# Raw buffers of their own for the modulation's weights, a fourth buffer for the high parts, and unread products in bfloat16

## The chip, the cores and the metric

The kernel runs on one core of a Trainium2 chip. The metric is the device time of one execution in microseconds (us). The kernel before was timed in 3 runs: 2639.55, 2638.19 and 2629.68 us, median 2638.19 us.

## The reference, cut to what matters

Two blocks are run one after the other in float32 on 256 tokens of 1024 channels. The first has two layers with four branches (RWKV-7, latent attention, a convolution, cross-attention to a memory). The second has two layers of a gated feed-forward, a mixed attention and another gated feed-forward, on the 256 tokens and on 256 context tokens. What each of its sublayers shifts, scales and gates is computed from the conditions `c` and `c_ctx` by one wide matrix per layer, the modulation:

```python
def first_block(x, ...):                      # two layers; every product has weights of its own
    for l in range(DEPTH):
        h = x @ w_in[l]
        ...
        merged = jnp.sum(gates * proj, axis=2)
        x = _layer_norm(DEEPNORM_ALPHA * x + merged @ w_out[l], ln_g[l], ln_b[l])
    return x

def swiglu(h, w1, w2):
    gate, up = jnp.split(h @ w1, 2, axis=-1)
    return (jax.nn.silu(gate) * up) @ w2

def ffn_sublayer(h, m, sub, g_pre, g_post, w1, w2):
    shift, scale, gate = mods_of(m, sub)
    y = swiglu(modulate(rms_norm(h, g_pre[sub]), shift, scale), w1, w2)
    return h + MACARON_WEIGHT * gate * rms_norm(y, g_post[sub])

def second_block(x, c, ctx, c_ctx, w_mod, b_mod, ...):
    xc = ctx
    c_act = jax.nn.silu(c)
    cc_act = jax.nn.silu(c_ctx)
    for layer in range(DEPTH):
        mod = (c_act @ w_mod[layer] + b_mod[layer]).reshape(b, 1, N_MOD, D_MODEL)
        mod_c = (cc_act @ w_mod[layer] + b_mod[layer]).reshape(N_MOD, D_MODEL)
        x, xc = hybrid_layer(x, xc, mod, mod_c, ...)   # ffn (sub 0), attention (sub 1), ffn (sub 2)
    return x
```

`mod` has 9 parts of 1024 numbers for each layer, three (shift, scale, gate) for each of the sublayers 0, 1 and 2. They depend on `c` alone, so they can be computed at any time before the sublayer that reads them.

## The kernel before, in words

**Weights.** All products are made in two parts, because TensorE multiplies a float32 operand rounded. A weight tile of 128 x 1024 float32 (512 KB) goes through `wload` (L178): SyncE (SP) issues a DMA into a raw buffer `wr` (pool of 4, L183), ScalarE (ACT) casts it to the high part `wh` (pool of 3, L175), and VectorE (DVE) subtracts to get the low part `wl` (pool of 3, L176). TensorE (PE) then makes three products for each pair of operands: high by high, high by low, low by high (`gemm`, L192). The kernel has 547 such tiles; they are numbered here in the order in which they are split. A tile of the feed-forward on 512 columns (256 tokens and 256 context tokens, tiles 240 to 300 for the first one) is 24 matmuls of 128x512. A raw buffer can be loaded again once its cast and its subtraction are done; a buffer of high parts, once TensorE has used it.

**Modulation.** It is computed in two ways. Layer 0's sublayer 0 goes through `mods` (L1212): 24 tiles of `wmod` are loaded in pairs, and TensorE multiplies them without a split; this runs beside the first block's second layer. The other five sublayers go through `mods_rows` (L1166), beside the second block: a 512 KB tile of the transposed matrix, `wmodT`, is fetched (L1173), and VectorE multiplies it by the row of silu(c) and sums along each row (L1188), once for the tokens and, in 88 of the 120 tiles, once more for the context. This document calls one such instruction a sum; there are 208. Each writes its 1024 products to `prod`, which is never read, and the sum to a column of `mm`, which is what counts. The fetch of the next tile stands right behind the sums of the last one. Both ways take their raw buffers from the same pool `wr` as the weights, and both are generators that `tick` (L214), called at the end of each `wload`, moves on by one step, so that their instructions are written between those of the tiles; `MODS_GAPS` sets after how many ticks the next tile follows.

**Order.** The program is compiled with a scheduler that moves instructions on each engine by its own costs and by when buffers come free; what it decides is then fixed. At run time each engine, and SP's queue of DMAs too, takes its instructions strictly in that order: one that waits holds up all behind it on its engine. Names in the rows: `ac`, `rw`, `sm` and `md` are PSUM accumulators; `blk`, `u`, `u2`, `u4`, `yout`, `pt` are tiles of activations; `ah` and `al` are the high and low parts of an activation.

**Lines.** L1224 is the fetch in `mods`, L1161 an activation in `c_rows` (L1154) that uses `prod` as a scratch tile, L1262 and L1275 open the second block's pools; the feed-forward's eviction is at L1466 to L1468.

Of the kernel before, what the change touches and what calls it, by code (L numbers as in the profile page):

```python
# [9 lines left out]
F32 = mybir.dt.float32  # L10
F32R = mybir.dt.float32r
BF16 = mybir.dt.bfloat16
I32 = mybir.dt.int32
AF = mybir.ActivationFunctionType
# [143 lines left out]
class Build:  # L158
    def __init__(self, tc, ap):
        self.tc, self.nc, self.ap = tc, tc.nc, ap  # L160
        self.bg = []
        self.ticks = 0
        self.modded = set()


# [11 lines left out]

    def wload(self, src, n, pieces=1):  # L178
        nc = self.nc
        raw = self.wr.tile([128, 1024], F32, name="wr")  # L180
        for p in range(pieces):
            sl = slice(p * n // pieces, (p + 1) * n // pieces)
            nc.sync.dma_start(out=raw[:, sl], in_=src[:, sl])  # L183
        h = self.wh.tile([128, 1024], F32R, name="wh")
        l = self.wl.tile([128, 1024], F32R, name="wl")
        for p in range(pieces):
            sl = slice(p * n // pieces, (p + 1) * n // pieces)
            self.split(h[:, sl], l[:, sl], raw[:, sl])
        self.tick()
        return h, l  # L190
# [43 lines left out]
    def build(self):  # L234
        nc, tc, ap = self.nc, self.tc, self.ap
        with ExitStack() as st:
            pool = lambda name, bufs, **k: st.enter_context(tc.tile_pool(name=name, bufs=bufs, **k))
            self.dr = pool("dr", 1, space=DRAM)
            self.wr = pool("wr", 4)
            self.wh = pool("wh", 3)  # L240
            self.wl = pool("wl", 3)
            c = self.c = pool("c", 1)
            self.ident = c.tile([128, 128], F32, name="ident")
            nc.scalar.dma_start(out=self.ident, in_=ap["ca"][:, 0:128])
            self.mhalf = c.tile([128, 16], F32, name="mhalf")
            nc.gpsimd.memset(self.mhalf, -0.5)
            self.ac = pool("ac", 2, space=PSUM)
            self.rw = pool("rw", 2, space=PSUM)
            self.sm = pool("sm", 3, space=PSUM)
            self.md = pool("md", 1, space=PSUM)  # L250
            self.accs = [self.ac]

            with ExitStack() as fin:
                with ExitStack() as s1:
                    self.first(fin, s1)
                self.second_open(st)
                self.finish(L - 1)
            self.second(st)


    def first(self, fin, st):
        nc, tc, ap = self.nc, self.tc, self.ap
        pool = lambda name, bufs, **k: st.enter_context(tc.tile_pool(name=name, bufs=bufs, side="right", **k))
        self.fin = fin.enter_context(tc.tile_pool(name="fin", bufs=1))
        self.ts = fin.enter_context(tc.tile_pool(name="ts", bufs=4))
        p1 = self.p1 = pool("p1", 1)
        self.ts.tile([128, 32], F32, name="pad3", bufs=1)
        self.f4 = fin.enter_context(tc.tile_pool(name="f4", bufs=7))
        self.xth = self.fin.tile([128, 8, 256], F32R, name="xth")
        self.xtl = self.fin.tile([128, 8, 256], F32R, name="xtl")  # L270
        self.ahead = []
        for k in range(0, 8, 2):
            xt = self.four((128, 2, 256))
            nc.sync.dma_start(out=xt, in_=ap["xT"][128 * k : 128 * k + 256].rearrange("(k p) t -> p k t", p=128))
            self.split(self.xth[:, k : k + 2], self.xtl[:, k : k + 2], xt)
            if k == 0:
                self.ahead.append(self.wload(ap["win"][0, :, 0:1024], 1024, 2))
        self.t1 = pool("t1", 2)
        self.t2 = pool("t2", 2)
        self.d2 = pool("d2", 16)  # L280
        self.d4 = pool("d4", 5)
        self.rp = pool("rp", 1)
        self.lw = p1.tile([128, 256], F32, name="lw")
        self.xd = self.dr.tile([256, 1024], F32, name="xd")
        for l in range(L):
            self.layer(l)
# [867 lines left out]
    def c_rows(self):  # L1154

        nc = self.nc
        self.cr = self.p2.tile([128, 2, 1024], F32, name="cr")
        self.prod = self.p2.tile([128, 1024], F32, name="prod")
        for r in range(2):
            nc.sync.dma_start(out=self.cr[:, r], in_=self.ap["cR"][r].partition_broadcast(128))  # L1160
            nc.scalar.activation(self.prod, self.cr[:, r], AF.Tanh, scale=0.5)  # L1161
            nc.vector.scalar_tensor_tensor(out=self.cr[:, r], in0=self.prod, scalar=1.0, in1=self.cr[:, r], op0=ALU.add,
                                           op1=ALU.mult)
            nc.vector.tensor_scalar(out=self.cr[:, r], in0=self.cr[:, r], scalar1=0.5, scalar2=None, op0=ALU.mult)

    def mods_rows(self, *which):  # L1166
# [2 lines left out]
        V = nc.vector  # L1169

        def fetch(l, sub, g):
            raw = self.wr.tile([128, 1024], F32, name="wr")
            nc.sync.dma_start(out=raw, in_=ap["wmodT"][l, sub, :, 1024 * g : 1024 * g + 1024])  # L1173
            return raw

# [36 lines left out]
    def mods(self, *which):  # L1212
# [3 lines left out]
        for l, sub in which:  # L1216
            for blk in range(6 * sub, 6 * sub + 6):
                m, half = blk // 2, slice(512 * (blk % 2), 512 * (blk % 2) + 512)
                ps = self.md.tile([128, 512], F32, name="md")
                for i in range(0, 4, 2):  # L1220
                    u = 4 * blk + i
                    raw = [self.wr.tile([128, 1024], F32, name="wr") for _ in range(2)]
                    for j in range(2):
                        nc.sync.dma_start(out=raw[j], in_=ap["wmod"][l, :, 1024 * (u + j) : 1024 * (u + j) + 1024])  # L1224
                    yield

                    for k in range(4):
                        self.mm(ps[32 * k : 32 * k + 32], self.cs[:, 2 * i + k],
                                raw[k // 2][:, 512 * (k % 2) : 512 * (k % 2) + 512], i == 0, i == 2)
                    yield  # L1230
                mr = self.wr.tile([128, 1024], F32, name="wr")
                A.copy(mr[:, 0:512], ps)
                for r in range(2):
                    nc.scalar.dma_start(out=self.ms[l, sub][r, :, m % 3, half], in_=mr[r:128:32, 0:512])
                yield

            q = self.wr.tile([128, 1024], F32, name="wr")
            nc.sync.dma_start(out=q[:, 0:80], in_=ap["pmod"][l, sub])
            gd = self.gd[l, sub]
            for r in range(2):  # L1240
# [21 lines left out]
    def second_open(self, st):  # L1262
        nc, ap = self.nc, self.ap
        pool = lambda name, bufs: st.enter_context(self.tc.tile_pool(name=name, bufs=bufs, side="right"))
        self.accs = [self.ac, self.rw]
        self.us = pool("us", 4)

        pool("pad", 1).tile([128, 48], F32, name="pad")
        self.xc = pool("xc", 1).tile([128, 2, 1024], F32, name="xc")
        nc.sync.dma_start(out=self.xc, in_=ap["ctx"].rearrange("(t p) d -> p t d", p=128))  # L1270
        self.u2 = pool("u2", 4)
        self.u4 = pool("u4", 3)
        self.blk = pool("blk", 5)

    def second(self, st):  # L1275
        nc, tc, ap = self.nc, self.tc, self.ap
        pool = lambda name, bufs, **k: st.enter_context(tc.tile_pool(name=name, bufs=bufs, **k))
        p2 = self.p2 = pool("p2", 1)
        p2.tile([128, 16], F32, name="pad2")
        self.ah = pool("ah", 4)  # L1280
        self.pt = pool("pt", 4)
        self.cb = p2.tile([128, NCB], F32, name="cb")
        nc.sync.dma_start(out=self.cb, in_=ap["cb"])
        for n, (a, b) in CB.items():
            setattr(self, n, self.cb[:, a:b])
        for l in range(L):
            last = l == L - 1
            if l == 0:
                self.c_rows()
                self.bg.append((self.mods_rows((0, 1), (0, 2), (1, 0), (1, 1), (1, 2)), 1))  # L1290
            self.ffn(l, 0, 0, (0, 1) if l else (1, 0), (l, 1))
            self.attention(l, last)
            self.ffn(l, 1, 2, (0,) if last else (0, 1), None if last else (l + 1, 0))
        for t in range(2):
            for c, queue in enumerate((nc.sync, nc.scalar)):
                sl = slice(512 * c, 512 * c + 512)
                queue.dma_start(out=ap["out"][128 * t : 128 * t + 128, sl], in_=self.X[0][t][:, sl])
# [535 lines left out]
```

## Time and profile before

| | |
|---|---|
| time, median of 3 runs | 2638.19 us (2629.68 to 2639.55) |
| the profiled execution's own time | 2642.53 us |
| its span, first to last instruction | 2640.7 us |
| mean granted TensorE clock | 0.989 |
| busy: PE, DVE, ACT, POOL | 2542.3, 1763.3, 1133.0, 231.2 us |
| DMA: moved, mean rate | 384.82 MB, 146 GB/s |
| DVE idle ahead of a sum, for its `wmodT` tile | 301.4 us, 93 times |

The profile gives for each engine the time in which it was busy, and for each instruction what ended the idle time before it. TensorE's matmuls are pipelined and their ends are modelled, so how far apart two matmuls start tells more than the length of one. The granted clock is full (1.00, the level of 2.4 GHz) or half (1.2 GHz); a stretch that mixes them shows a mean between.

### The profile page before, as it was taken

The page shows a single profiled execution, that of the slowest core. Times are in us where ns is not written, and L with a number is a line of the kernel's source. Part 1 is how long each engine was busy: PE and PEld are TensorE (multiplying, and loading weights), DVE is VectorE, ACT ScalarE, POOL GpSimd, SP SyncE. Part 2 cuts the span into 40 slices and gives each one's busy share as a digit, 9 for nine tenths or more (in the row PEclk, how much of TensorE's full clock was granted, in tenths as well). Part 3 has the DMA queues.
Part 4 walks back from the last instruction along what each step waited for, and adds up shares of the span by engine and source line. Part 5 has one row for each costly group of instructions (what it writes and reads, how often), then busy time and mean ns, then how long its engine had stood idle before and what let it go on. Part 6 is the DMA issues. An engine that isn't in the chain of part 4 may idle for free.

```text
span 2640.7 us, 42329 instructions
## 1 busy us (share of the span) xinstructions
PE 2542.3 (96%) x16658; PEld 2167.7 (82%) x16658; DVE 1763.3 (67%) x3066; ACT 1133.0 (43%) x1936; POOL 231.2 (9%) x245
## 2 busy tenths in 40 slices
PE   8999999998999899999899999999999999899998
PEld 7888998877899888887766788887788888766997
DVE  7988667797766785557777575656654445655656
ACT  5365454444545532233546342223432234545445
POOL 1121101112111100000212010000000000111000
PEclk9999999999999999999999999999999999999999
DMA  6344466545547654444441244444445543322564
GB/s 206 105 120 137 131 207 217 155 134 194 158 121 217 199 185 138 152 158 145 128 128 56 82 153 157 147 155 143 146 147 157 160 128 96 96 80 85 171 185 151
DMA packets 124712, 384.82 MB, mean 146 GB/s; under 512 B 28352, under 2 KB 32176, under 8 KB 124384
## 3 DMA queue, kind: packets, MB, share of 16 engines
q1 hardware_dynamic: 121504, 380.19, 47.2%
q8 instruction: 131, 2.15, 0.3%
q10 hardware_dynamic: 3008, 1.92, 0.2%
q14 instruction: 69, 0.57, 0.1%
HBM read 379.80 MB, written 2.26 MB: 145 GB/s over the span
## 4 chain that ended last, share of the span: by engine, by line
PE 71%; DVE 13%; DMA 7%; issue 4%; ACT 2%; POOL 1%; DVEq 0%; SPq 0%; POOLq 0%; ACTq 0%
PE ac L167 37%; PE rw L167 20%; PE sm L167 10%; DMA wr<-in_wmodT 6%; DVE wl L176 4%; PE md L167 2%; PE sm L170 2%; DVE prod L1188 2%; DVE br L816 2%; DMA wr<-in_win 1%; ACT wh L175 1%; POOL rs L204 1%; DVE blk L1351 0%; DVE br L1424 0%; PE rw L170 0%
## 5 line engine op out<-in xcount | busy, mean ns | idle before, releaser
L175 ACT CAST wh<-wr 128x1024 fp32r<-128x1024 f32 (+2 forms) x547 | 569.0, 1041 | 852.7 <-PE ac L167 388.2
L176 DVE TENSOR_TENSOR wl<-wr,wh 128x1024 fp32r<-128x1024 f32 (+2 forms) x547 | 696.9, 1275 | 240.0 <-ACT wh L175 237.3
L1188 DVE CUSTOM_DVE_ANT_0 prod<-wr,cr 128x1024 f32<-128x1024 f32 x208 | 254.2, 1222 | 302.5 <-DMA wr<-in_wmodT 301.4
L167 PE MATMUL rw<-blk,wh 128*128 128x512 f32 (+1 forms) x1600 | 424.6, 350 | 4.2 <-DVE blk L1350 3.8
L167 PE MATMUL ac<-blk,wh 128*128 128x512 f32 (+1 forms) x1552 | 412.9, 351 | 2.6 <-DVE blk L1350 1.8
L167 PE MATMUL ac<-xth,wh 128*128 128x256 f32 x1248 | 356.9, 286 | 7.6 <-ACT wh L175 5.3
L167 PE MATMUL ac<-xth,wl 128*128 128x256 f32 x1248 | 350.1, 281 | 2.6 <-DVE wl L176 2.4
L167 PE MATMUL ac<-xtl,wh 128*128 128x256 f32 x1248 | 349.4, 280 | 0.1
L167 PEld LDWEIGHTS rw<-blk,wh 128*128 128x128 f32 x1600 | 283.3, 189 | 45.0 <-DVE blk L1350 4.7
L167 PEld LDWEIGHTS ac<-blk,wh 128*128 128x128 f32 x1552 | 275.6, 190 | 42.0 <-DVE blk L1350 2.3
L167 PE MATMUL rw<-blk,wl 128*128 128x512 f32 (+1 forms) x800 | 279.7, 350 | 4.5 <-DVE wl L176 4.5
L167 PE MATMUL ac<-blk,wl 128*128 128x512 f32 (+1 forms) x776 | 272.2, 351 | 1.1 <-DVE wl L176 1.1
L167 PEld LDWEIGHTS ac<-xth,wh 128*128 128x128 f32 x1248 | 236.2, 189 | 18.1 <-issue 7.6
L167 PEld LDWEIGHTS ac<-xth,wl 128*128 128x128 f32 x1248 | 235.9, 189 | 5.6 <-DVE wl L176 4.2
L167 PEld LDWEIGHTS ac<-xtl,wh 128*128 128x128 f32 x1248 | 236.1, 189 | 2.5 <-issue 1.5
L175 ACT CAST ah<-blk 128x512 fp32r<-128x512 f32 (+1 forms) x170 | 95.8, 566 | 195.7 <-PE sm L167 98.6
L167 PEld LDWEIGHTS rw<-blk,wl 128*128 128x128 f32 x800 | 151.0, 189 | 25.1 <-DVE wl L176 5.7
L167 PEld LDWEIGHTS ac<-blk,wl 128*128 128x128 f32 x776 | 146.9, 189 | 21.2 <-DVE wl L176 1.9
L176 DVE TENSOR_TENSOR al<-blk,ah 128x512 fp32r<-128x512 f32 (+1 forms) x170 | 103.9, 619 | 64.7 <-ACT ah L175 64.6
L816 DVE SCALAR_TENSOR_TENSOR br<-hp,pv,br 128x256 f32<-128x256 f32 x240 | 113.8, 508 | 0.9
L167 PE MATMUL ac<-f,wh 128*128 128x256 f32 x640 | 113.9, 280 | 0.0
L204 POOL TENSOR_TENSOR rso<-rso,mhalf 128x1 f32<-128x1 f32 x20 | 15.5, 773 | 1001.8 <-DVE rso L1419 1001.8
(440 smaller groups left out, 4257.9 us busy)
## 6 DMA issues: line engine op xcount, KB each, us to landing
wr<-in_w SPq DMA_DIRECT2D x264, 512.0 KB
wr<-in_win SPq DMA_DIRECT2D x187, 512.0 KB
wr<-in_wmodT SPq DMA_DIRECT2D x120, 512.0 KB
wr<-in_wo SPq DMA_DIRECT2D x32, 512.0 KB
wr<-in_wout SPq DMA_DIRECT2D x32, 512.0 KB
wr<-in_wmod SPq DMA_DIRECT2D x24, 512.0 KB
wr<-in_wkv SPq DMA_DIRECT2D x16, 512.0 KB
gate<-gd SPq DMA_DIRECT2D x10, 512.0 KB
```

Source lines behind the costliest of these rows:

```text
L167: self.nc.tensor.matmul(out, a, b, start=start, stop=stop, skip_group_check=True)
L170: self.nc.tensor.transpose(out, a, self.ident[:n, :n])
L175: nc.scalar.copy(h, src)
L176: (eng or nc.vector).tensor_tensor(out=l, in0=src, in1=h.bitcast(F32), op=ALU.subtract)
L204: self.nc.gpsimd.tensor_tensor(out=out, in0=in_, in1=self.mhalf[:p, :n], op=ALU.pow)
L816: V.scalar_tensor_tensor(out=acc, in0=hp[:, j : j + 256], scalar=w(j), in1=acc, op0=ALU.mult, op1=ALU.add)
L1188: V.tensor_tensor_reduce(out=self.prod, in0=raw, in1=self.cr[:, r], scale=1.0, scalar=0.0, op0=ALU.mult, op1=ALU.add, accum_out=m[:, g, r ...
```

## The change

Three things are changed. The pool of raw buffers has 3 instead of 4, and that of high parts 4 instead of 3; in the first block every fourth weight tile goes to one more raw buffer, `wx`, which is dropped when the second block is opened. The modulation takes its tiles from a pool of its own: 2 buffers (`w0`) in `mods`, 1 buffer (`wm`) in `mods_rows`. And the products that nobody reads, `prod`, become bfloat16 (the scratch of `c_rows` moves to a `yout` tile).

```diff
@@ Build.__init__
+        self.wx, self.turn = None, 0
@@ wload
-        raw = self.wr.tile([128, 1024], F32, name="wr")
+        self.turn = (self.turn + 1) % 4
+        raw = (self.wx if self.wx and self.turn == 0 else self.wr).tile([128, 1024], F32, name="wr")
@@ build
-            self.wr = pool("wr", 4)
-            self.wh = pool("wh", 3)
+            self.wr = pool("wr", 3)
+            self.wh = pool("wh", 4)
@@ first
+        self.wx = pool("wx", 1)
+        self.wm = pool("w0", 2)
@@ c_rows
-        self.prod = self.p2.tile([128, 1024], F32, name="prod")
+        tmp = self.yout().rearrange("p a t -> p (a t)")
+        self.prod = self.p2.tile([128, 1024], BF16, name="prod")
@@ mods_rows, fetch
-            raw = self.wr.tile([128, 1024], F32, name="wr")
+            raw = self.wm.tile([128, 1024], F32, name="wm")
             nc.sync.dma_start(out=raw, in_=ap["wmodT"][l, sub, :, 1024 * g : 1024 * g + 1024])
@@ mods
-                    raw = [self.wr.tile([128, 1024], F32, name="wr") for _ in range(2)]
+                    raw = [self.wm.tile([128, 1024], F32, name="wr") for _ in range(2)]
...
-                mr = self.wr.tile([128, 1024], F32, name="wr")
+                mr = self.wm.tile([128, 1024], F32, name="wr")
...
-            q = self.wr.tile([128, 1024], F32, name="wr")
+            q = self.wm.tile([128, 1024], F32, name="wr")
@@ second_open
+        self.wx = None
@@ second
+        self.wm = pool("wm", 1)
```

The scheduler also writes the instructions in another order. Three places follow; in the rows, a number behind a name tells one tile from another, and a line of after stands 2 to 7 higher than the same line of before.

SP's queue in the first feed-forward of the second block, around weight tile 253, before:

```order
L183 DMA wr_12122<-in_w1 128x1024
L1173 DMA wr_12130<-in_wmodT 128x1024
L183 DMA wr_12157<-in_w1 128x1024
L183 DMA wr_12192<-in_w1 128x1024
L1173 DMA wr_12200<-in_wmodT 128x1024
L183 DMA wr_12227<-in_w1 128x1024
```

The same queue at the same tile, after:

```order
L185 DMA wr_12134<-in_w1 128x1024
L1178 DMA wm_12072<-in_wmodT 128x1024
L185 DMA wr_12169<-in_w1 128x1024
L1178 DMA wm_12142<-in_wmodT 128x1024
L185 DMA wr_12204<-in_w1 128x1024
L1178 DMA wm_12212<-in_wmodT 128x1024
L185 DMA wr_12239<-in_w1 128x1024
```

Fetches and weight loads stand about 2 to 3 before and 1 to 1 after, and a fetch stands behind a later weight load than it did (`wm_12142` behind tile `wr_12169`; before, the same tile of the modulation, `wr_12130`, behind `wr_12122`).

VectorE at the same place, before (rows with `mm` alone read the sum out):

```order
L176 TENSOR_TENSOR wl_12125<-wr_12122,wh_12124 128x1024
L1188 ISA prod_11354,mm_11380<-wr_12200,cr_11353 128x1024
L1188 ISA mm_11380 128x1
L176 TENSOR_TENSOR wl_12160<-wr_12157,wh_12159 128x1024
L1467 SCALAR_TENSOR_TENSOR u2_12118<-u2_12118,ac_12062 128x512
L1188 ISA prod_11354,mm_11380<-wr_12235,cr_11353 128x1024
L1188 ISA mm_11380 128x1
L1188 ISA prod_11354,mm_11380<-wr_12235,cr_11353 128x1024
L1188 ISA mm_11380 128x1
```

And after:

```order
L177 TENSOR_TENSOR wl_12137<-wr_12134,wh_12136 128x1024
L1193 ISA prod_11366,mm_11392<-wm_12212,cr_11364 128x1024
L1193 ISA mm_11392 128x1
L1193 ISA prod_11366,mm_11392<-wm_12212,cr_11364 128x1024
L1193 ISA mm_11392 128x1
L177 TENSOR_TENSOR wl_12172<-wr_12169,wh_12171 128x1024
L1474 SCALAR_TENSOR_TENSOR u2_12130<-u2_12130,ac_12074 128x512
L1193 ISA prod_11366,mm_11392<-wm_12247,cr_11364 128x1024
L1193 ISA mm_11392 128x1
L1475 SCALAR_TENSOR_TENSOR blk_11376<-u2_12130,rw_12105 128x512
L177 TENSOR_TENSOR wl_12207<-wr_12204,wh_12206 128x1024
L1193 ISA prod_11366,mm_11392<-wm_12247,cr_11364 128x1024
```

Between tiles 240 and 300 VectorE has 76 sums before and 104 after; a pair of sums on one tile of the modulation now stands at nearly each weight tile, with one or two other instructions between a pair's end and the next pair.

VectorE at the end of the first attention of the second block (weight tile 319), before:

```order
L176 TENSOR_TENSOR ah_14096<-sm_15700,al_14095 128x256
L1721 SCALAR_TENSOR_TENSOR blk_14089<-sm_15739,blk_14089 128x256
L1721 SCALAR_TENSOR_TENSOR blk_14089<-sm_15746,blk_14089 128x256
L176 TENSOR_TENSOR ah_14096<-sm_15778,al_14095 128x256
L176 TENSOR_TENSOR wl_15864<-wr_15861,wh_15863 128x1024
L1188 ISA prod_11354,mm_15770<-wr_15995,cr_11353 128x1024
```

And after:

```order
L1193 ISA prod_11366,mm_17534<-wm_17456,cr_11364 128x1024
L1193 ISA mm_17534 128x1
L177 TENSOR_TENSOR ah_14108<-sm_15712,al_14107 128x256
L1728 SCALAR_TENSOR_TENSOR blk_14101<-sm_15751,blk_14101 128x256
L1728 SCALAR_TENSOR_TENSOR blk_14101<-sm_15758,blk_14101 128x256
L1193 ISA prod_11366,mm_17534<-wm_17540,cr_11364 128x1024
L1193 ISA mm_17534 128x1
L1193 ISA prod_11366,mm_17534<-wm_17540,cr_11364 128x1024
L1193 ISA mm_17534 128x1
L177 TENSOR_TENSOR ah_14108<-sm_15790,al_14107 128x256
L177 TENSOR_TENSOR wl_15876<-wr_15873,wh_15875 128x1024
L1193 ISA prod_11366,mm_17534<-wm_17610,cr_11364 128x1024
```

There, between tiles 310 and 320, VectorE has 12 sums before and 32 after. The last sum stands at tile 434 before and at tile 369 after.

## Rows read from the trace of the kernel before

**Rows 1.** The page: engines' busy time, and the chain that ended last.

```profile
PE 2542.3 (96%) x16658; PEld 2167.7 (82%) x16658; DVE 1763.3 (67%) x3066; ACT 1133.0 (43%) x1936; POOL 231.2 (9%) x245
...
PE 71%; DVE 13%; DMA 7%; issue 4%; ACT 2%; POOL 1%; DVEq 0%; SPq 0%; POOLq 0%; ACTq 0%
```

**Rows 2.** Waits, whole program: engine, line, releaser; us in total, times, longest.

```profile
DVE prod L1188 <- DMA wr<-in_wmodT: 301.4, 93, 6.7
```

**Rows 3.** Waits of SP's own queue, whole program.

```profile
SPq L183 <- DMA wr<-in_wmodT: 170.1, 59, 4.5
```

**Rows 4.** Waits of DVE between 930 and 1212 us (tiles 239 to 290).

```profile
DVE prod L1188 <- DMA wr<-in_wmodT: 100.4, 26, 6.7
DVE wl L176 <- ACT wh L175: 1.3, 3, 0.8
```

**Rows 5.** Busy time by stretch: PE, PEld, DVE, ACT, POOL (instructions), PEclk, DMA share, GB/s.

```profile
500.00:700.00 200.00, 184.40 (x1819) 154.41 (x1818) 170.34 (x400) 91.90 (x185) 40.61 (x49) 0.98 0.51 163
930.00:1212.00 282.00, 276.29 (x1211) 226.10 (x1209) 179.80 (x258) 78.63 (x97) 0.14 (x1) 1.00 0.50 157
1212.00:1340.00 128.00, 118.99 (x586) 99.90 (x586) 98.83 (x148) 58.78 (x103) 13.99 (x9) 0.97 0.50 148
1340.00:1483.00 143.00, 140.68 (x676) 93.00 (x676) 94.71 (x297) 79.97 (x197) 27.21 (x23) 1.00 0.24 69
1483.00:1512.00 29.00, 29.00 (x129) 23.81 (x128) 14.14 (x19) 7.65 (x15) 0.57 (x1) 1.00 0.42 135
1610.00:1770.00 160.00, 160.00 (x708) 132.38 (x707) 94.31 (x136) 39.29 (x46) 0.14 (x1) 1.00 0.48 152
1770.00:1830.00 60.00, 56.23 (x240) 45.12 (x239) 38.49 (x56) 21.51 (x30) 0.00 (x0) 0.97 0.50 151
1895.00:1910.00 15.00, 11.56 (x62) 9.80 (x62) 12.82 (x26) 9.93 (x22) 3.22 (x4) 0.89 0.35 106
```

**Rows 6.** DVE's groups by shape: count | busy us, mean ns | idle before.

```profile
L1188 DVE CUSTOM_DVE_ANT_0 prod<-wr,cr 128x1024 f32<-128x1024 f32 x208 | 254.2, 1222 | 302.5 <-DMA wr<-in_wmodT 301.4
...
L1467 DVE SCALAR_TENSOR_TENSOR u<-u,ac 128x512 f32<-128x512 f32 x44 | 29.9, 680 | 1.9 <-ACT u L1466 1.9
```

**Rows 7.** SP's DMA issues from 975 us: start, us, line (x2: two issues merged).

```profile
981.39 0.33 SPq L1173 DMA_DIRECT2D wr<-in_wmodT  x1
983.13 4.84 SPq L183 DMA_DIRECT2D wr<-in_w  x2
988.78 0.33 SPq L1173 DMA_DIRECT2D wr<-in_wmodT  x1
```

**Rows 8.** DVE in order of time, near 985 and 2501 us: start, us, [idle before <-releaser].

```profile
981.28 0.08 DVE L1188 DVE_READ_ACCUMULATOR2_ANT mm<- 128x1 f32 x1
...
985.11 1.23 DVE L1188 CUSTOM_DVE_ANT_0 prod<-wr,cr 128x1024 f32<-128x1024 f32 x1 [2.01 <-DMA wr<-in_wmodT]
...
987.53 1.22 DVE L176 TENSOR_TENSOR wl<-wr,wh 128x1024 fp32r<-128x1024 f32 x1
...
993.99 1.23 DVE L1188 CUSTOM_DVE_ANT_0 prod<-wr,cr 128x1024 f32<-128x1024 f32 x1 [4.64 <-DMA wr<-in_wmodT]
...
2501.53 1.23 DVE L176 TENSOR_TENSOR wl<-wr,wh 128x1024 fp32r<-128x1024 f32 x1 [0.54 <-ACT wh L175]
```

**Rows 9.** PE in order of time, near 1210 and 1825 us.

```profile
1210.60 0.50 PE L167 MATMUL ac<-wl,ah 128*128 128x512 f32 x1 [2.84 <-DVE wl L176]
...
1212.95 0.80 PE L167 MATMUL ac<-wh,al 128*128 128x512 f32 x1 [0.78 <-DVE al L176]
...
1825.80 0.51 PE L167 MATMUL rw<-wl,ah 128*128 128x512 f32 x1 [3.12 <-DVE wl L176]
```

**Rows 10.** ACT in order of time, last feed-forward.

```profile
2500.45 1.05 ACT L175 CAST wh<-wr 128x1024 fp32r<-128x1024 f32 x1 [1.50 <-PE rw L167]
...
2508.93 1.05 ACT L175 CAST wh<-wr 128x1024 fp32r<-128x1024 f32 x1 [1.78 <-PE ac L167]
...
2511.75 1.05 ACT L175 CAST wh<-wr 128x1024 fp32r<-128x1024 f32 x1 [1.50 <-PE rw L167]
```

More of the change, by code (lines that the diff above doesn't have):

```diff
@@ L1157, in c_rows @@
         self.cr = self.p2.tile([128, 2, 1024], F32, name="cr")
-        self.prod = self.p2.tile([128, 1024], F32, name="prod")
+        tmp = self.yout().rearrange("p a t -> p (a t)")
+        self.prod = self.p2.tile([128, 1024], BF16, name="prod")
         for r in range(2):
             nc.sync.dma_start(out=self.cr[:, r], in_=self.ap["cR"][r].partition_broadcast(128))
-            nc.scalar.activation(self.prod, self.cr[:, r], AF.Tanh, scale=0.5)
-            nc.vector.scalar_tensor_tensor(out=self.cr[:, r], in0=self.prod, scalar=1.0, in1=self.cr[:, r], op0=ALU.add,
+            nc.scalar.activation(tmp, self.cr[:, r], AF.Tanh, scale=0.5)
+            nc.vector.scalar_tensor_tensor(out=self.cr[:, r], in0=tmp, scalar=1.0, in1=self.cr[:, r], op0=ALU.add,
                                            op1=ALU.mult)
```

## The prediction, made before the run

> **What bounds the kernel now.** First the page: TensorE is busy for 96% of the span and the chain that ended last runs through it for 71% [rows 1]. What the change can give back is therefore no more than TensorE's idle time and half clock, and what it can cost is whatever makes TensorE wait longer. Then the waits: VectorE idles 301.4 us ahead of the modulation's sums, for a `wmodT` tile [rows 2], and weight loads stand in SP's queue for 170.1 us behind such a tile's buffer [rows 3]. Most of that costs TensorE nothing as long as VectorE keeps its place, so I read by stretch. From 930 to 1212 us VectorE waits 100.4 us for `wmodT` and 1.3 us for anything else [rows 4]: it never waits for the casts, so it is late already, its queue being sums, subtractions and waits for fetches. TensorE still loses only 282 - 276.29 = 5.7 us there [rows 5], much of it in one place, 2.84 + 0.78 us at 1210 [rows 9]. So in the first feed-forward of the second block VectorE and TensorE run side by side with next to no slack; there the change puts more sums. From 1610 to 1770 TensorE is busy throughout; 160 us / 708 = 0.226 us per matmul, and 24 of them make 5.4 us per weight tile [rows 5].
>
> **Single buffer in the first feed-forward (tiles 240 to 300).** The order has 104 sums in 60 tiles, 52 fetches, where it had 76. With one buffer a fetch can only start when the second sum on the last tile has read it. A cycle is then: the sum read out at 981.28 + 0.08, the issue at 981.39, 0.33 us long, so the DMA leaves at 981.72 and its sum starts at 985.11: 3.39 us; two sums from 985.11 to 987.53: 2.42 us [rows 7, 8]. Together 0.03 + 0.33 + 3.39 + 2.42 = 6.2 us, above the 5.4 us of a weight tile. What VectorE does between a pair and the next (a subtraction of 1.22 us, an eviction of 0.68 [rows 6, 8]) lies inside the 3.39 us. But in about nine pairs such work stands between the two sums, and there it lengthens the cycle by 1.22 + 0.68 = 1.9 us, 17 us in all. 52 x 6.2 + 17 = 339 us, against 60 x 5.4 = 325 us of TensorE and, with the 4 us at 1210, about 329 us before: **+10 us**. From below: if VectorE's lead at the start (up to two low parts, 11 us) covers it, 0. From above: the tile issued at 988.78, about 1 us behind a weight load, starts its sum at 993.99, 4.9 us after its issue ends [rows 7, 8]; a cycle of 7.7 us would give 52 x 7.7 + 17 - 329 = +88 us. I take the lower landing, because in the new order the fetch stands directly ahead of the weight load that waits for the next subtraction, as at 981.39 (the two loads behind it begin at 983.13), and not behind it.
>
> The Trainium skill ("DMA: Bandwidth & Descriptors", Anatomy of one DMA) gives a fixed 2.0 us plus bytes / 436 GB/s for a DMA issued from GpSimd. For 512 KB that is an estimate of 3.2 us, near the 3.39 us seen on SP's queue; the sum by it would be 10 us lower, so no loss in this stage. It says nothing of the 4.9 us seen behind another load, and the trace has both.
>
> **Transition and attention (tiles 300 to 330).** At tile 300 the order has one pair more, 2.4 us and a wait on a path where TensorE already loses 128 - 118.99 = 9.0 us [rows 5]: +3 us (0 to +6). Between tiles 310 and 320 there are 32 sums for 12: 20 x 1.22 = 24 us of work and ten more fetches of up to 3.4 us exposed, 58 us at most. VectorE's idle time there is 172 - 108.9 = 63 us of the stretch from 1340 to 1512, and TensorE loses only 2.3 us in it [rows 5]. Much of that idle time is at the end, where the high and low parts of the output wait for one another, and there the new order puts four pairs back to back with three to five short instructions between, each with its fetch bare. Four pairs at 5.8 us less the hidden work and the idle time that was there leave some 14 us: **+14 us** (0 if the idle time takes it all, +35 if the pairs stand bare before the projection). Behind that, to tile 369, there is one sum per weight tile, and a cycle of 6.2 us for two tiles is hidden in 10.8: 0.
>
> **What goes.** Behind tile 369 no sums are left. At 1825.80 TensorE waits 3.12 us for a low part, and the stretch to 1830 loses 3.8 us and 0.03 x 60 = 1.8 us of clock [rows 5, 9]: -6 us (bounds -6 and 0). From 1895 to 1910 TensorE idles 3.4 us, with VectorE busy 12.8 of 15 us [rows 5] and one sum among it: -2 us. Beside the first block's second layer, weight loads no longer stand behind the modulation's pairs in one ring and stand 3 to 4 tiles ahead in the order instead of 1; TensorE idles 15.6 us between 500 and 700 [rows 5], a third of which I give to it: -5 us (-12 to +5, since SP's queue is in order and a pair now waits there for TensorE to have read the last one). Each new gap of over 3 us also drops the clock to half for a while, as before 1830: three new gaps at 1.8 us: +5 us.
>
> **What costs nothing.** Three raw buffers in the last feed-forward: a cast comes every 2.82 us and a subtraction ends at 2502.76; with four buffers the next load into it is cast at 2511.75, with three at 2508.93 [rows 8, 10]. That leaves 6.2 us, above the 4.9 us of the slowest landing used here; without that cover, each of its narrow tiles would wait. The fourth high part lets a cast run one tile earlier, but in this part casts wait for TensorE and nothing waits for them: 0. bfloat16 products: a sum takes 1222 ns for 1024 columns [rows 6], the same as a subtraction of two float32 tiles, so I read one column per cycle set by the two float32 inputs: 0, and -0.6 us per sum at best.
>
> The sum against the profiled execution's 2642.5 us: 10 + 3 + 14 - 6 - 2 - 5 + 5 = +19, that is 2661.5 us. That execution was 4.3 us above the median of the runs, 2638.2 us, so **2657 us** beside that median.
>
> **Rivals.**
> *The fetch hides at last (faster).* The buffer is the modulation's own, so a fetch no longer waits in a ring for a weight tile's subtraction, and a weight load no longer waits for a sum. For it: 301.4 and 170.1 us of waits [rows 2, 3]. Against it: one buffer is one fetch in flight at best, and never under a sum. If lead and idle time hide the three additions, what goes is left, and with it 1210 and half of the idle time from 1212 to 1340: -13 - 6 - 5 = -24, beside the median 2614 us.
> *Contended landing (much slower).* The single buffer's cycle is not 6.2 us but midway to the row of 4.9 us, 6.9 us: 52 x 6.9 + 17 - 329 = +47 in place of +10, so about 2694 us. It decides from a landing of 4 us on; the row at 988.78 is for it.
> *All of it beside TensorE (no change).* 96% busy, and the losses and the gains are of one size: 2638 us. For it: TensorE lost only 5.7 us in 282 with VectorE late throughout.
> *Cheaper sums.* The Trainium skill ("VectorE: DVE Perf Modes", Terms) has the engine pick its mode from the operands' types and alignment, with more than one result per cycle from 16 bits; no row here shows a sum with a 16-bit output. As a mechanism of this kernel: a sum of 0.6 us makes the cycle 5.0 us, 52 x 5.0 + 17 = 277 us, below TensorE's 325, so it ends like the first rival, about 2612 us. The two inputs stay float32, which speaks against it.
>
> **How the numbers follow.** Forecast as worked out 0.42, with a range of its own of 2643 to 2674; contended 0.14; no change 0.20; fetch hides 0.19; cheaper sums 0.05. About 0.5%, 13 us, is what a measurement of this kernel can tell from no change. The forecast's range reaches 8 of its 42 hundredths into that band. So faster 0.19 + 0.05 = 0.24; same 0.20 + 0.08 = 0.28; slower 0.34 + 0.14 = 0.48. The range, 2612 to 2694 us, leaves out the longer half of the contended case and a little of the faster ones.
>
> **What would show it.** Right: between tiles 240 and 300 VectorE's waits for `wm` grow in number to about 52, each near 1.5 us (3.4 less 1.9 of hidden work), TensorE gets waits for `wl` there (over 10 us) and the stage grows from 329 to about 339 us; from tile 310 to 320 TensorE's idle time grows from 2 to about 16 us; behind tile 369 VectorE waits for nothing of the modulation, and the gap at 1825 is gone. Wrong: sums of 0.6 us; a fetch that lands over 4 us after its issue throughout; SP's weight loads waiting for raw buffers in the last feed-forward; or a first feed-forward as long as before, whose VectorE waits for casts.

## The result, and the profile after

The changed kernel takes 2652.4 us (median of 5 runs, 2646.0 to 2655.7), the kernel before 2638.19 us (median of 5, 2629.68 to 2641.25). The ratio is 1.0052, 95% interval 1.0034 to 1.0070: half a per cent slower. The profiled execution took 2650.9 us with a span of 2649.1 us, 8.4 us more than the one of before.

Page of after, busy time and the chain that ended last, to be held against [rows 1]:

```profile
PE 2547.8 (96%) x16658; PEld 2170.9 (82%) x16658; DVE 1754.7 (66%) x3066; ACT 1133.2 (43%) x1936; POOL 248.5 (9%) x245
...
PE 59%; DVE 9%; DMA 8%; issue 3%; POOL 1%; ACT 1%; DVEq 0%; POOLq 0%; ACTq 0%; SPq 0%
```

Waits of after, whole program (engine, line, releaser; us in total, times, longest), to be held against [rows 2]:

```profile
DVE prod L1193 <- DMA wm<-in_wmodT: 150.6, 94, 3.4
ACT wh L176 <- DMA wr<-in_w: 145.7, 68, 6.1
```

VectorE's wait for the modulation's tiles is halved, 301.4 us in 93 times to 150.6 in 94, and the kernel is slower. The sum of a wait over the program says nothing here; the stretch does.

TensorE runs the same products in nearly the same order in all these kernels, so the start of the same matmul in two traces can be subtracted. What a kernel gains or loses on before from one milestone to the next (us, worked out that way; times at the head are those of before, columns are stretches, and `end` is the total):

```
                          to 456 456-667 667-700 700-937 937-1271 1271-1331 1331-1512 1512-1770 1770-1843 1843-2451 2451-2575  end
after                        0.0    -3.5    +7.0    -4.4    +12.8      -1.0     +10.7      +0.3      -7.8      -1.4      -4.7  +8.0
own_buffer_wr4_wh3          +1.1    -5.7    -1.1    +1.8    +15.3      -0.8      +8.5      +3.5      -7.8      -1.7       0.0 +13.2
three_high_parts            -0.4    -5.9    -1.2    -1.3    +12.5      +1.4      +5.1      +1.2      -7.8      -2.0       0.0  +1.6
two_buffers_wh3             -1.1    -7.1    -0.7    +0.8     +4.1      -3.5      +6.3      -3.1      -7.8      -1.8       0.0 -13.9
paced_one_buffer            +2.2    -3.5    +5.9    -5.3     -7.8      -0.6      +5.2      +2.1      -7.8      +1.1       0.0  -8.5
paced_three_high_parts      +1.4    -8.2    -0.5    +1.6     -6.3      +5.1      +7.9      +1.8      -7.8      -0.8      -4.6 -10.2
paced_two_buffers           -0.3    -5.9    -0.5    +1.7    -10.6      -2.0      +5.0      +4.9      -7.8      -2.7      -4.6 -22.9
one_sum_per_fetch           +0.4    -7.0    +7.0    -4.5    -10.4      -4.6      +3.0      +0.4      -7.8      +1.4      -4.6 -26.8
before_bf16_only            +1.2    +0.8    -0.2    +5.2     -4.6      -2.1      +2.8      -0.3       0.0      +0.3      -4.6  -1.4
```

The first row is the result; the others are the experiments below. The first feed-forward of the second block (937 to 1271) lost 12.8 us, the attention (1331 to 1512) 10.7 us, a place at 667 to 700 7 us; 1770 to 1843 and the last feed-forward gave back 7.8 and 4.7 us. The last row shows how far one profile can be trusted: `before_bf16_only` runs TensorE's products in exactly the order of before, and yet its stretches differ from before's by up to 5.2 us. An entry of that size in a single profile is not to be put down to a change; 12.8 us is well clear of it, and -7.8 us comes out alike in eight kernels. One column does not go with the change at all: in 2451 to 2575 each kernel shows either 0 or -4.6 us, and `before_bf16_only` shows -4.6 (last section). Without it the profile's difference is 12.7 us, close to the medians' 14.2.

Busy time of after by stretch (columns as in [rows 5]); the second row is the first feed-forward, the fourth the attention:

```profile
660.00:700.00 40.00, 35.19 (x274) 31.21 (x271) 27.39 (x69) 16.67 (x33) 4.74 (x4) 0.91 0.41 122
936.00:1283.00 347.00, 332.69 (x1430) 268.44 (x1429) 247.22 (x362) 99.41 (x130) 0.28 (x2) 0.99 0.55 170
1283.00:1342.00 59.00, 51.16 (x298) 44.40 (x297) 49.48 (x76) 32.24 (x62) 17.74 (x9) 0.97 0.45 126
1342.00:1534.00 192.00, 186.47 (x845) 128.71 (x844) 142.31 (x374) 90.44 (x215) 28.91 (x24) 0.96 0.37 113
1792.00:1852.00 60.00, 60.00 (x266) 49.72 (x265) 26.20 (x32) 23.23 (x35) 0.00 (x0) 1.00 0.31 92
```

The same matmuls of the first feed-forward in before:

```profile
937.00:1271.00 334.00, 327.51 (x1430) 268.27 (x1429) 215.79 (x308) 100.67 (x132) 0.14 (x1) 0.99 0.50 158
```

334 us became 347, TensorE's idle time in it went from 6.5 us to 14.3; the rest shows as longer matmuls beside the waits (busy 332.7 us against 327.5), of which about 1.7 us are half clock: the trace's records of the granted clock have 6.8 us at the lower level here in after and 3.4 in before. Who it waits for, and whom VectorE waits for (after, 936 to 1283 us):

```profile
PE ac L168 <- DVE wl L177: 6.7, 7, 1.3
PE ac L168 <- DVE al L177: 6.2, 6, 2.2
```

```profile
DVE prod L1193 <- DMA wm<-in_wmodT: 95.4, 49, 3.4
```

49 waits of 95.4 / 49 = 1.95 us each, for 51 tiles of the modulation (102 sums in this trace between tiles 240 and 300, two fewer than the 104 given with the change). The cycle can be read off VectorE in order of time (after):

```profile
1103.03 1.23 DVE L1193 CUSTOM_DVE_ANT_0 prod<-wm,cr 128x1024 bf16<-128x1024 f32 x1 [2.02 <-DMA wm<-in_wmodT]
1104.18 0.08 DVE L1193 DVE_READ_ACCUMULATOR2_ANT mm<- 128x1 f32 x1
1104.30 1.22 DVE L1193 CUSTOM_DVE_ANT_0 prod<-wm,cr 128x1024 bf16<-128x1024 f32 x1
1105.45 0.08 DVE L1193 DVE_READ_ACCUMULATOR2_ANT mm<- 128x1 f32 x1
1105.45 1.22 DVE L177 TENSOR_TENSOR wl<-wr,wh 128x1024 fp32r<-128x1024 f32 x1
1106.59 0.68 DVE L1474 SCALAR_TENSOR_TENSOR u<-u,ac 128x512 f32<-128x512 f32 x1
1109.51 1.23 DVE L1193 CUSTOM_DVE_ANT_0 prod<-wm,cr 128x1024 bf16<-128x1024 f32 x1 [2.24 <-DMA wm<-in_wmodT]
...
1115.62 1.23 DVE L1193 CUSTOM_DVE_ANT_0 prod<-wm,cr 128x1024 bf16<-128x1024 f32 x1 [1.27 <-DMA wm<-in_wmodT]
...
1121.72 1.23 DVE L1193 CUSTOM_DVE_ANT_0 prod<-wm,cr 128x1024 bf16<-128x1024 f32 x1 [1.86 <-DMA wm<-in_wmodT]
```

And SP's issues at that time (after):

```profile
1105.56 0.33 SPq L1178 DMA_DIRECT2D wm<-in_wmodT  x1
1106.70 0.33 SPq L185 DMA_DIRECT2D wr<-in_w  x1
1112.04 0.33 SPq L1178 DMA_DIRECT2D wm<-in_wmodT  x1
```

The sum's read-out ends at 1105.53, the fetch is issued at 1105.56 to 1105.89, and the next sum starts 3.6 us later, at 1109.51; the next one 3.25 us after its issue ends (1112.37 to 1115.62). These three cycles are 6.5, 6.1 and 6.1 us long, against 5.4 us of TensorE's weight tile [rows 5], and the one subtraction that TensorE needs lies inside each.

Worked out in the same way from SP's issues and VectorE's rows, the 51 cycles of the stretch follow one another without a break, each fetch issued 0.03 us behind the last read-out. From 939.47 on they take 347.1 us, as long as the whole stretch: 6.8 us each. 31 of them take 6.0 to 6.7 us. Of the 20 longer ones eleven have other work of VectorE between the two sums, eight a late landing, and in one VectorE was busy elsewhere when the tile came. The eight are the fetches that were issued 1.1 to 1.7 us behind a weight load: their sum starts 4.4 to 4.7 us after the issue ends. The fetches issued 3 us or more behind one took 3.2 to 4.0 us, apart from the one for which VectorE was busy.

### The profile page after: what moved, and what is told of

Same layout as the page of the kernel before. It is cut to its first block, busy times and chain, and to the rows that moved or that the text cites. A ratio compares the mean times of both kernels' runs of the same rounds, so it can differ in the third digit from the quotient of the medians.

```text
span 2649.1 us, 42312 instructions
## 1 busy us (share of the span) xinstructions
PE 2547.8 (96%) x16658; PEld 2170.9 (82%) x16658; DVE 1754.7 (66%) x3066; ACT 1133.2 (43%) x1936; POOL 248.5 (9%) x245
## 4 chain that ended last, share of the span: by engine, by line
PE 59%; DVE 9%; DMA 8%; issue 3%; POOL 1%; ACT 1%; DVEq 0%; POOLq 0%; ACTq 0%; SPq 0%
PE ac L168 27%; PE rw L168 19%; PE sm L168 9%; DMA wm<-in_wmodT 8%; DVE prod L1193 4%; PE md L168 3%; PE sm L171 2%; DVE wl L177 1%; DVE br L820 1%; POOL rs L206 1%; DVE br L1431 0%; DVE u L1338 0%; POOL rso L206 0%; DVE u L1424 0%; DMA wr<-in_wmod 0%
## 5 line engine op out<-in xcount | busy, mean ns | idle before, releaser
L177 DVE TENSOR_TENSOR wl<-wr,wh 128x1024 fp32r<-128x1024 f32 (+2 forms) x547 | 681.3, 1247 | 318.3 <-issue 120.2
L1193 DVE CUSTOM_DVE_ANT_0 prod<-wm,cr 128x1024 bf16<-128x1024 f32 x208 | 254.6, 1224 | 152.6 <-DMA wm<-in_wmodT 150.6
L168 PEld LDWEIGHTS ac<-blk,wl 128*128 128x128 f32 x776 | 147.3, 190 | 25.7 <-DVE wl L177 6.5
```

What stands on the lines that cost most here:

```text
L168: self.nc.tensor.matmul(out, a, b, start=start, stop=stop, skip_group_check=True)
L177: (eng or nc.vector).tensor_tensor(out=l, in0=src, in1=h.bitcast(F32), op=ALU.subtract)
L1193: V.tensor_tensor_reduce(out=self.prod, in0=raw, in1=self.cr[:, r], scale=1.0, scalar=0.0, op0=ALU.mult, op1=ALU.add, accum_out=m[:, g, r ...
```

## Experiments

All are compared with before, and their stretches are in the table above. "Paced" means one added instruction: GpSimd copies one column of the newest weight tile's low part into the modulation's buffer ahead of its fetch, so that the fetch depends on that tile.

**Pacing alone** (`paced_one_buffer`):

```diff
@@ wload
             self.split(h[:, sl], l[:, sl], raw[:, sl])
+        self.cur = l
         self.tick()
@@ mods_rows, fetch
             raw = self.wm.tile([128, 1024], F32, name="wm")
+            nc.gpsimd.tensor_copy(raw[:, 0:1], self.cur[:, 0:1].bitcast(F32))
             nc.sync.dma_start(out=raw, in_=ap["wmodT"][l, sub, :, 1024 * g : 1024 * g + 1024])
```

> The changed kernel, but GpSimd writes one column of the modulation's buffer from the newest weight tile's low part ahead of each fetch, so that a fetch can't be issued earlier than its place in the program; the order then has 74 sums between tiles 240 and 300 (102 in the changed kernel, 76 before), 14 between 310 and 320 (32, 12), the last one at tile 438 (369, 434). One buffer, three raw, four high parts stay. Theory A (the time is lost where the single buffer meets more sums per weight tile): the first feed-forward of the second block gives back its 12.8 us, the attention about 10 of its 12, the 8 us gained at 1825 are lost again, the narrow tiles keep their gain: about 2635 us, 15 to 20 below the changed kernel. Theory B (three raw buffers instead of four make weight loads late): unchanged, 2650 us.

Measured: 2630.3 us, ratio to before 0.9962 (0.9946 to 0.9977): 0.4% faster. The first feed-forward takes 7.8 us less than in before, 20.6 less than in the changed kernel; TensorE is busy 324.05 of 326 us in it:

```profile
936.00:1262.00 326.00, 324.05 (x1429) 267.53 (x1428) 213.76 (x303) 99.33 (x130) 22.26 (x38) 1.00 0.49 160
```

With three raw buffers the loss is gone, so theory B falls, and one buffer does no harm where it is used 37 times in 60 tiles. Three parts of the expectation were wrong: the attention gave back 5 us, not 10, the 7.8 us at 1770 stayed although sums stand there again, and the narrow tiles did not keep their gain (0.0 in the table).

**Own buffers, with four raw and three high parts** (`own_buffer_wr4_wh3`):

```diff
-            self.wr = pool("wr", 3)
-            self.wh = pool("wh", 4)
+            self.wr = pool("wr", 4)
+            self.wh = pool("wh", 3)
-        self.wx = pool("wx", 1)
```

> The changed kernel with four raw buffers and three high parts as before and no wx; the modulation keeps buffers of its own (2 and 1), the products bfloat16. Its order has the same 102 sums between tiles 240 and 300 and 30 between 310 and 320. Theory A: both losses stay (first feed-forward about 340 us, attention +12), and the 4.6 us that the narrow tiles gained go if the fourth high part was their cause: 2652 to 2657 us. Theory B: the losses go, 2630 to 2638 us.

Measured: 2645.15 us, ratio 1.0025 (1.0011 to 1.0038). The time lies between the ranges of the two theories, so it decides nothing; the profile does, of an execution that took 2655.72 us. Four raw buffers do not take the loss away: the first feed-forward is 15.3 us longer than in before, with the same waits:

```profile
DVE prod L1192 <- DMA wm<-in_wmodT: 100.8, 50, 3.6
```

**Two buffers** (`two_buffers_wh3`):

```diff
-            self.wh = pool("wh", 4)
+            self.wh = pool("wh", 3)
-        self.wm = pool("wm", 1)
+        self.wm = pool("wm", 2)
```

> The changed kernel with two buffers for the modulation in the second block and three high parts. The order takes the sums further ahead: 165 between tiles 240 and 300, the last at tile 318. Theory A, the single buffer's latency being what makes a cycle longer than a weight tile: with it gone VectorE has some 5 us of work in each weight tile of 5.4 us, so the first feed-forward stays near 330 us, the attention loses 5 us, nothing behind it has a sum: about 2640 us. Rival (VectorE's work ahead of the subtractions costs, with any number of buffers): the first feed-forward grows by over 20 us, 2660 us or more.

Measured: 2628.64 us, ratio 0.9956 (0.9942 to 0.9971). The first feed-forward costs 4.1 us over before, no more than two executions of one order differ by, with more than twice its sums, and VectorE is busy 322 of 338 us:

```profile
929.00:1267.00 338.00, 329.59 (x1427) 267.63 (x1427) 322.12 (x493) 97.90 (x129) 0.41 (x3) 0.99 0.73 223
```

Its waits for the modulation's tiles there are nearly gone:

```profile
DVE prod L1193 <- DMA wm<-in_wmodT: 11.8, 32, 0.9
```

So the amount of work ahead of the subtractions is not what cost 12.8 us; the wait for the one buffer was. The time came out 11 us better than expected; about 7 us of that is the shorter first block (-8.1 up to 937, where the changed kernel has -0.9; three high parts, below), the rest is spread over the stretches behind it.

**The products in bfloat16 alone** (`before_bf16_only`):

```diff
-        self.prod = self.p2.tile([128, 1024], F32, name="prod")
+        tmp = self.yout().rearrange("p a t -> p (a t)")
+        self.prod = self.p2.tile([128, 1024], BF16, name="prod")
```

> The kernel before with the unread products in bfloat16 alone (and the scratch of the activation in a yout tile): the order is that of before. All theories: a sum takes 1.22 us as before and the time is that of before, within 0.3%. A rival on the narrow tiles of the last feed-forward (2.82 us each before, 2.72 after): if the pace differs from run to run and not from kernel to kernel, this profile may show either.

Measured: 2646.02 us, ratio 1.0022 (1.0003 to 1.0041): within the 0.3%, though the interval just leaves out no change. A sum is as long as before [rows 6], with the same wait:

```profile
L1189 DVE CUSTOM_DVE_ANT_0 prod<-wr,cr 128x1024 bf16<-128x1024 f32 x208 | 254.2, 1222 | 302.3 <-DMA wr<-in_wmodT 301.2
```

**Three high parts** (`three_high_parts`), the changed kernel with `pool("wh", 3)`:

> The changed kernel with three high parts instead of four (three raw buffers and wx, own buffers for the modulation of 2 and 1, bfloat16 products as in it). Two profiles with four high parts show VectorE held 4.5 us at 670 by the last readback of the first block's modulation, TensorE 4.5 us behind it and then at half clock; two with three high parts do not. Theory: that comes with the fourth high part's order, so here the first block is some 10 us shorter, the two losses of the second block (12.8 us in the first feed-forward, about 10 in the attention) stay: 2640 to 2646 us. Rival (the 7 us at 670 came by chance of an execution): 2652 us.

Measured: 2646.44 us, ratio 1.0033 (1.0013 to 1.0052), just above what the theory gave; the interval overlaps that of the changed kernel, so the gain is shown in the trace and not by the times. Both halves of the theory hold there: the first feed-forward keeps its loss (+12.5). At 667 to 700 the 7 us are gone in all five kernels with three high parts and the modulation's own buffers, and there in all three with four. In the changed kernel VectorE waits 4.55 us in the last step of `mods` for its readback (the row names no releaser; the chain that ended last comes to it from the transfer issued at 664.95), and TensorE 4.48 us behind it, held by VectorE's `ge`, a transfer that follows it and the cast behind that:

```profile
670.51 0.49 DVE L1250 TENSOR_REDUCE wr<-wr 128x48 f32<-128x192 f32 x1 [4.55 <-issue]
```

```profile
677.92 1.65 PE L168 MATMUL sm<-e,e 96*128 96x128 f32 x5 [4.48 <-ACT e L1026]
```

In all three kernels with four high parts this reduction stands on VectorE ahead of the work on `ge`; in the five with three it stands behind, and VectorE does not wait for it. So the loss comes with the order that the scheduler wrote; why that goes with the number of buffers no run tells. With three high parts TensorE is busy throughout the same work:

```profile
655.00:695.00 40.00, 40.00 (x362) 35.36 (x361) 33.57 (x77) 20.58 (x41) 4.81 (x4) 1.00 0.50 139
```

**Paced, three high parts** (`paced_three_high_parts`), the first and the fifth edit together:

> The paced kernel (fetches no earlier than their place in the program, one buffer) with three high parts. Theory: both gains add, 2630 - 10 = 2620 us (2616 to 2626), no TensorE gap of over 2 us near 670. Rival (the fourth high part is what made the paced kernel faster): 2630 us or more.

Measured: 2632.79 us, ratio 0.9984 (0.9967 to 1.0002). The expectation failed: the gains did not add. At 700 this kernel is 12 us ahead of the paced one with four high parts, but the latter makes up 7 of them by 937, and from 1271 to 1512 this one loses 13.0 us on before, the other 4.6. One row of TensorE shows much of it:

```profile
1301.01 0.58 PE L168 MATMUL rw<-blk,wh 128*128 128x256 f32 x1 [6.28 <-DVE blk L1360]
```

This is no wait for a fetch. The VectorE instruction that TensorE waits for took 7.16 us, ten times the 0.69 us of the same operation at 1292.64, while GpSimd made an addition of 128x3072:

```profile
1293.79 7.16 DVE L1360 TENSOR_TENSOR blk<-u,blk 128x512 fp32r<-128x512 f32 x1
```

```profile
1293.65 6.76 POOL L1508 TENSOR_TENSOR blk<-blk,cb 128x3072 f32<-128x3072 f32 x1 [5.25 <-DMA blk<-in_rpb]
```

TensorE's granted clock has a mean of 0.83 from 1295 to 1315. VectorE does wait for the modulation's only buffer, four times from 1255 to 1370, but once at 1260 (2.98 us) and otherwise behind 1325, so that the buffer caused the row above is not shown:

```profile
DVE prod L1195 <- DMA wm<-in_wmodT: 15.6, 4, 4.9
```

**Paced, two buffers** (`paced_two_buffers`), the same with `pool("wm", 2)`:

> The paced kernel with three high parts and two buffers for the modulation in the second block. Theory: at 72 sums in 60 tiles one buffer is no limit, so the second brings nothing: within 0.2% of the paced kernel with three high parts, about 2620 us. Rival (a fetch that lands under the sums of the one before always helps): 5 us or more below it.

Measured: 2620.13 us, ratio 0.9937 (0.9913 to 0.9960), 12.7 us below the paced kernel with three high parts and one buffer, and the intervals do not meet: the rival's number was right. Its reason is not shown. 7.1 of the 12.7 us lie between 1271 and 1331, where GpSimd's addition now meets a subtraction of a weight tile (7.43 us at 1294.37) and TensorE waits 0.58 us behind it instead of 6.28; whether the second buffer moved VectorE there, or the order did, is open. The 4.3 us in the first feed-forward are no more than two executions of one order differ by. VectorE's wait for the modulation's tiles does fall, from 163.3 to 32.2 us in the whole program:

```profile
L1195 DVE CUSTOM_DVE_ANT_0 prod<-wm,cr 128x1024 bf16<-128x1024 f32 x208 | 254.0, 1221 | 34.8 <-DMA wm<-in_wmodT 32.2
```

By the medians this version beats both kernels: 18 us below before, 32 below the changed one. In its first feed-forward VectorE waits for casts (52.1 us, 48 times) and hardly for fetches (7.3 us, 8 times).

**One sum on each tile** (`one_sum_per_fetch`), which leaves out the context's part of the modulation:

```diff
-            for r in range(2 if both(g) else 1):
+            for r in range(1):
```

> The changed kernel without the second sum on each tile of the modulation (the context's modulation isn't computed, so part of the computation is left out). The single buffer and the lead of the order stay: 59 fetches between tiles 240 and 300. The cycle becomes 0.03 + 0.33 + 3.39 + 1.21 = 5.0 us, below a weight tile's 5.4. Theory (cycle against weight tile): TensorE's time from tile 240 to 300 is within 4 us of before, no waits of TensorE for low parts there. Rival (any fetch that waits for the last sum costs): the 12.8 us stay.

Measured: 2615.76 us in a single run, so the trace counts and not the time. The single buffer and the order's lead are there (59 waits in the stretch), and TensorE loses nothing; the stretch is 10.4 us shorter than in before, which idles in it, where within 4 us was expected:

```profile
933.00:1257.00 324.00, 324.00 (x1431) 268.22 (x1430) 202.19 (x277) 99.21 (x130) 0.28 (x2) 1.00 0.67 197
```

```profile
DVE prod L1193 <- DMA wm<-in_wmodT: 54.8, 59, 3.2
```

So a fetch that waits for the last sum costs nothing here, where the cycle fits into a weight tile: the shortest cycles take 4.8 to 5.0 us, and all 60 together 324.2 us, 5.4 each, because it is now VectorE that waits for the stage (25.7 us for TensorE's results at L1475 alone). The edit also takes work from VectorE, but `two_buffers_wh3` shows that this work is not the cause. That is the test of the forecast's central step, and it holds.

## Why the prediction was right, and where not

The sign, the range and the size hold: 2657 us forecast, 2652.4 measured. The central step, the single buffer's cycle, is shown by experiment; the other terms missed by 1 to 5 us in both directions and largely cancelled, and that is luck. By steps:

- **The single buffer in the first feed-forward: right.** Forecast 52 cycles of 6.2 us and 17 us of work between sums, 339 us and +10; measured 51 cycles in 347.1 us and +12.8, and +15.3 and +12.5 in two more kernels with as many sums there. Pacing, a second buffer and a shorter cycle each take it away. The bare cycle alone would have fitted, 52 x 6.2 = 322 us against 325: the loss lies in the cycles that were longer. The 17 us were met by luck: twelve pairs had work between the sums, not nine, at 0.5 to 1.6 us each, not 1.9, and every pair took 2.50 us with its last read-out, not 2.42. The forecast had no late landings; the sums that started later than 3.39 us behind the issue add 15 us. The contended rival is out as the rule, but eight fetches of 51, those right behind a weight load, were the case that it describes. Of the signs named, TensorE's waits for `wl` were 6.7 us and not over 10; with those for `al` they are 12.9.
- **Transition: forecast +3, measured -1.0.** The extra pair at tile 300 cost nothing that shows. Here too GpSimd's addition comes in: in before the subtraction under it took 6.43 us and TensorE waited 2.58 us behind it at 1314.27, in after it waited for none, so +3 may be hidden in this.
- **Attention: too large, and in the wrong place.** Forecast +14, from four pairs at its end; measured +10.7, with the one long stall near the beginning (TensorE waits 3.0 us for VectorE at 1369.92) and the rest clock: a mean of 0.96 over 192 us is 7.7 us. The two kernels with nearly the same order of sums lost 8.5 and 5.1 us there, the paced ones with 12 to 14 sums between tiles 310 and 320 5.0 to 7.9, before's own order in another execution 2.8. So at most a few microseconds are the sums'. What the others share is half clock: by the trace's records TensorE ran 17.1 us of this stretch at the lower level in after, 3.4 to 10.2 in the eight other kernels and none in before. Half of that, and what its idle time grew by, comes within 1.1 us of each kernel's entry. Why the clock fell in one execution and not in the other was not settled.
- **1825: right in size (-6, measured -7.8), wrong in reason.** I put it to the sums being over. In the paced kernels sums stand there up to tile 438, and the 7.8 us are gained all the same; with bfloat16 alone they are not. What goes is most of VectorE's wait for these tiles, which share no buffers with the weight loads any more. VectorE's waits for the modulation's tiles from 1770 to 1830 in before, and from 1740 to 1830 in the paced kernel with one buffer:

```profile
DVE prod L1188 <- DMA wr<-in_wmodT: 21.0, 6, 4.3
```

```profile
DVE prod L1195 <- DMA wm<-in_wmodT: 5.6, 5, 1.7
```

- **1895 (-2): in 1843 to 2451 the changed kernel gains 1.4.**
- **Three new gaps at half clock (+5): too small, and not by gaps.** TensorE idles for over 3 us as often as before (four times after the first 10 us in either trace). Half clock still takes 78.5 us of the program instead of 54.6, its last piece left out; half of the difference, 12 us, is an estimate of its cost. 17.1 of the 78.5 us are those of the attention, counted there, and 6.8 those behind the stall at 677.92.
- **First block's modulation: the term -5 was the sum of two that I did not see.** Own buffers gave 6 to 9 us up to 700 wherever three high parts were kept; the fourth high part, put at 0 ("casts wait for TensorE and nothing waits for them"), cost 6 to 7 us at 667 with an order that puts the readback's wait in front of TensorE; 4 to 5 of them came back by 937, which those kernels with three did not show. The sentence was argued for the last feed-forward only.
- **Three raw buffers in the last feed-forward: right that they cost nothing.** TensorE does not idle from 2470 to 2600. But casts there wait for loads (48.4 us in 34 waits, up to 2.3 us) where before they waited for TensorE; the forecast had every load land ahead of its cast. With three high parts they wait for TensorE alone (68.8 us from 2450 to 2590 in `three_high_parts`). SP's weight loads do wait for raw buffers there, which was named as a sign of being wrong (111 us in 48 waits from 2470 to 2600), but they did so in before (120 us in 46), so the sign tells nothing.
- **bfloat16: right**, 1224 ns against 1222.

The sum +19 on the profile was +8.4, or about +13 without the pace of the last section; beside the medians it was +14.2, since the profiled execution of before lies 4.3 us above its median and that of after 1.5 below. The forecast was nearer than its terms.

## What to carry to other kernels

A buffer of its own frees a side stream from the main ring, but one buffer makes it serial: transfer plus work, with nothing of the two overlapping. Compare all its cycles with the stage that it runs beside (here 51 of 6.8 us against 60 weight tiles of 5.4), work between and late landings included, before giving it more to do, and remember that a scheduler gives it more as soon as buffers come free. Where memory allows only few buffers, hold the stream to its rate with a dependency. In these runs a second buffer for the stream went with a lower time than a fourth for the high parts (2620 us against 2630, both paced), though what made the difference was not shown.

## What the runs showed of the hardware that was not expected

The narrow matmuls of the last feed-forward (128x256) run at one of two paces at a granted clock of 1.00, and which one does not go with the order of the instructions. Before and after, the same stretch of 55 us, columns as above:

```profile
2500.00:2555.00 55.00, 55.00 (x469) 55.00 (x468) 30.74 (x39) 23.34 (x29) 0.00 (x0) 1.00 0.63 185
```

```profile
2500.00:2555.00 55.00, 55.00 (x488) 55.00 (x487) 32.38 (x42) 23.89 (x30) 0.00 (x0) 1.00 0.66 194
```

55 us hold 469 matmuls in one and 488 in the other, 117 ns against 113, without idle time; five of the ten profiles show the slow pace, five the fast one, and the kernel with before's order shows the fast one, before the slow one. It is worth 4.6 us and was not forecast. What sets it was not found; each kernel has one profile, so whether it differs between executions of one kernel is not shown either. A difference of one pair of profiles in such a stretch is not to be put down to a change.

VectorE is held up while GpSimd adds. In each of the ten traces one VectorE instruction with two operands takes 5.5 to 7.8 us while GpSimd adds 128x3072 numbers in 6.8 to 8.0 us ahead of the first attention, and ends 1.1 us behind that addition (0.5 us in `paced_three_high_parts`), just short of its own usual length. In nine it is a subtraction of a weight tile (1.22 us elsewhere), and TensorE waits up to 3.3 us behind it; in `paced_three_high_parts` it is the low part of an activation (L1360), and TensorE waits 6.28 us.
